# Channel mixers: one product, the plain blocks' last product and their low parts moved to GpSimd, and a third down slab converted later

## The chip, the cores and the metric

The kernel runs on one core of one Trainium2 chip. The metric is the time of one execution on the device, in microseconds (us); lower is better. The core's engines work from queues of their own, each in order: TensorE (PE) multiplies matrices, ScalarE (ACT) applies functions and converts, VectorE (DVE) and GpSimd (POOL) work element by element, and SyncE (SP) issues the transfers (DMA) from the large memory. An engine that needs another's result waits on a semaphore, and everything behind the waiting instruction in its own queue waits with it.

## The reference

A decoder trunk of two layers on 512 tokens of width 1024, all in float32. Each layer runs a channel mixer, a token mixer (latent attention in the first layer, sparse attention in the second) and a second channel mixer; a last norm closes the trunk.

```python
def rmsnorm(x, g):
    y = x32 * lax.rsqrt(jnp.mean(x32 * x32, axis=-1, keepdims=True) + RMS_EPS)
    return y.astype(x.dtype) * g
def swiglu(x, w_gate, w_up, w_down):
    return (jax.nn.silu(x @ w_gate) * (x @ w_up)) @ w_down
...
  h = h + 1/2 * SwiGLU_a(RMSNorm(h))
  h = h + Mixer_i(RMSNorm(h))
  h = h + 1/2 * SwiGLU_b(RMSNorm(h))
```

So there are four channel mixers (idx 0 to 3 below), with 2816 hidden values each. The change touches only these.

## The kernel before

**Two parts for each number.** Every float32 factor is kept as a high part, rounded by a copy on ACT (L176), and a low part, the difference, subtracted on DVE (L177); `split` makes both, and its argument `pool=True` gives the subtraction to POOL. A product takes three matmuls, high by high, high by low and low by high (`mm3`, `product`, `plain`).

**Blocks.** A channel mixer works through 22 blocks f of 128 hidden values, with all 512 tokens in the free dimension. The first 3 blocks of idx 0, and the first 2 of the others, are plain: gate and up are multiplied out directly (`plain`, L379 to L381) into the banks pg and pu. The others take one turn of the main loop each, in which gate and up together are made by seven half-sized products of sums (a Strassen scheme) in the order 1, 7, 6, 2, 5, 4, 3, into three banks px, pq and pg. `wsums` makes five weight sums for a later turn on DVE (L353, L354, L356, L357) from the raw slabs wr (called rg there) and ru and splits them. Within a turn ACT copies px to pg after product 1 (L496; product 6 then goes on in px, so PE waits for that copy), then pq and px to uq (L498, L500), and px to pg after product 5 (L503). DVE adds up the up half in tile tu (L504, L506).

**Activation.** `row` is a tile 128x512 that holds every token's norm factor. `gate` multiplies the gate by row (DVE, L395), applies silu with a turned sign (ACT, L396, tile tg) and multiplies the result by row once more (DVE, L397); that second product brings in the factor that the up half lacks. `act` multiplies tu by tg (L408 on DVE; for plain blocks L406, which reads the bank pu and turns the sign) and splits the result into ah (ACT) and al (DVE). `plain_acts` does both for the plain blocks, and stands behind the weight sums of the first turn.

**Down.** For every three finished blocks there are eight units, one for each 128 rows of the output: `unit` loads a down slab wdr (L425, SP), splits it into two wd tiles (ACT and DVE), runs nine matmuls into bank pd (L168 to L170) and adds the result to h (L419). They are spread over the next three turns as 3, 3 and 2, with the bank tags "o", "T" and "S"; only a turn's third unit has the tag "S". From `tail` = 18 on, the last blocks' turns are spread otherwise.

**What orders the work.** A scheduler places every instruction on its engine's queue from its own estimates. `issue_after(x)` keeps what it encloses behind instruction x on that engine. The tag "w2" (tu) has two buffers, "dr" (wdr) two, "wr" two, "dh" and "dl" (wd) three.

Of the kernel before, what the change touches and what calls it, by code (L numbers as in the profile page):

```python
# [14 lines left out]
AF = mybir.ActivationFunctionType  # L15
ALU = mybir.AluOpType
AX = mybir.AxisListType

P = 128
S = 512  # L20
# [27 lines left out]
HS = S // 2  # L48
# [16 lines left out]
class Kern:  # L65
# [317 lines left out]
    def ffn(self, idx, gain_next, ap, tp):  # L383
        nc, a = self.nc, self.a
        self.scr, self.fp = (tp, "sq", 1), tp
        ah, al, ht, plain = {}, {}, [], PLAIN[idx]
        self.nsum = 0
        ap.tile([P, 3 * PAD], F32, name="even")
        tp.tile([P, 5 * PAD], F32, name="odd", bufs=1)
        tg, tu, units = {}, {}, []  # L390

        def gate(f, g):

            t = tg[f] = tp.tile([P, S], F32, tag="tg", bufs=2, name="tg")
            nc.vector.tensor_tensor(t, g, row, op=ALU.mult)  # L395
            nc.scalar.activation(t, t, AF.Silu, scale=-1.0)  # L396
            nc.vector.tensor_tensor(t, t, row, op=ALU.mult)  # L397

        def tu_tile():
            return self.xp.tile([P, S], F32, tag="w2", bufs=2, name="tu")  # L400

        def act(f):
            t = tu[f]
            if f < plain:
                t = tu_tile()
                nc.vector.scalar_tensor_tensor(t, tu[f], -1.0, tg[f], op0=ALU.mult, op1=ALU.mult)  # L406
            else:
                nc.vector.tensor_tensor(t, t, tg[f], op=ALU.mult)  # L408
            ah[f] = ap.tile([P, S], F32R, tag="act", bufs=4 * NG, name="ah")
            al[f] = ap.tile([P, S], F32R, tag="act", bufs=4 * NG, name="al")  # L410
            self.split(t, ah[f], al[f])

        def down(p, w, b0, b1):
            for k in range(b0, b1):
                last = self.mm3(p, w[0][:, k - b0], w[1][:, k - b0], ah[k], al[k], k == b0, k == b1 - 1)
            return last

        def add(c, p):
            nc.vector.scalar_tensor_tensor(self.h[c], p, 0.5, self.h[c], op0=ALU.mult, op1=ALU.add)  # L419

        def unit(tag, b0, c):

            w = [ap.tile([P, NG * P], F32R, tag=t, bufs=3, name="wd").rearrange("p (k c) -> p k c", c=P) for t in ("dh", "dl")]
            raw = ap.tile([P, NG * P], F32, tag="dr", bufs=2, name="wdr")
            nc.sync.dma_start(raw, a["w_down"][idx, c, :, b0 * P : (b0 + NG) * P])  # L425
            self.split(raw.rearrange("p (k c) -> p k c", c=P), *w)
            p = self.bank(tag, "pd")
            down(p, w, b0, b0 + NG)
            add(c, p)

        sums, xts = self.small_sums, []

        def tokens(t):

            xts.append(tp.tile([P, D], F32, tag="fr", bufs=3, name="xt"))
            with self.tc.issue_after(self.high.ins):
                nc.scalar.dma_start(xts[t], a["x_tok"][t * P : (t + 1) * P, :])

        def squares(t):
            nc.scalar.activation(xts[t], xts[t], AF.Square, accum_out=sums[:, t : t + 1])  # L440

        if idx == 0:
            for t in range(3):
                tokens(t)


        def plain_acts():
            for e, g in enumerate(gates):
                gate(e, g)
                act(e)  # L450
            t = self.tiny
            for i, g in enumerate(gates[::-1]):
                nc.scalar.activation(t[:, i + 1 : i + 2], g[:, 0:1], AF.Identity, bias=t[:, i : i + 1])

        row = self.row_tile(tp, tag="row", bufs=1)
        gates = [self.bank("T", "pg") for _ in range(plain)]
        for f, g in enumerate(gates):
            u = tu[f] = self.bank(("mm", "S")[f % 2], "pu")
            self.plain(idx, f, 0, g)
            if f == 0 and idx:  # L460
                with self.tc.high_priority(URGENT):
                    for c in self.late:
                        self.sumsq(self.h[c])
                self.norm_col(D, self.s2, URGENT, col=row[:, 0:P:32])
                self.norm_row(row, URGENT)
            if f == 1 and idx == 0:

                squares(0)
                tokens(3)
                squares(1)  # L470
            self.plain(idx, f, 1, u)
            if f == 1 and idx == 0:
                squares(2)
                squares(3)
                self.rsqrt_col(sums, D, col=row[:, 0:P:32])
                self.norm_row(row)
            for p in (((0, 1), (2, 3)) if plain == 2 else ((0, 1), (2,), (3,)))[f]:
                self.combine(p)

        tail, left = (NF - 2) // NG * NG, 1  # L480
        for f in range(plain, NF):
            if f % NG == 0 and f <= tail:
                units = [partial(unit, b0=f - NG, c=c) for c in range(KC)]
                left = NG if f < tail else NF - tail
            n = -(-len(units) // left)
            left -= 1
            todo, units = units[:n], units[n:]
            w = self.wsums(idx, f)
            if f == plain:
                plain_acts()  # L490
            x, q, g = self.bank("S", "px")[:, :HS], self.bank("mm", "pq")[:, :HS], self.bank("T", "pg")
            uq = tp.tile([P, S], F32, tag="uq", bufs=1, name="uq")
            t = tu[f] = tu_tile()

            self.product(1, w, x, True, False)
            nc.scalar.activation(g[:, :HS], x, AF.Copy)  # L496
            self.product(7, w, q, True, False)
            nc.scalar.activation(uq[:, :HS], q, AF.Copy)  # L498
            self.product(6, w, x, False, False)
            nc.scalar.activation(uq[:, HS:], x, AF.Copy)  # L500
            self.product(2, w, g[:, :HS], False, True)
            self.product(5, w, x, False, True)
            nc.scalar.activation(g[:, HS:], x, AF.Copy)  # L503
            nc.vector.tensor_tensor(t[:, HS:], x, uq[:, :HS], op=ALU.add)  # L504
            self.product(4, w, q, False, True)
            nc.vector.tensor_tensor(t[:, :HS], q, uq[:, HS:], op=ALU.add)  # L506
            self.product(3, w, g[:, HS:], False, True)
            gate(f, g)
            for work, tag in zip(todo, "oTS"):
                work(tag)  # L510
            act(f)
        if gain_next == "fin":

            hs, out = [self.parts(self.four(F32)) for _ in range(4)], []
            for t in range(4):
                for b in range(2):
                    p = self.mm_bank("ph")
                    for c in range(4):
                        nc.tensor.transpose(p[:, c * P : (c + 1) * P], self.h[4 * b + c][:, t * P : (t + 1) * P], self.ident)
                    out.append(hs[t][b])  # L520
                    nc.scalar.activation(out[-1], p, AF.Copy)
            return self.last(a["w_last"], ah, al, ap, out, hs)
        self.norm_begin(gain_next)
        for c in self.order:
            p = self.mm_bank("pd")
            raw = tp.tile([P, D], F32, tag="fr", bufs=3, name="wdr")[:, : (NF - tail) * P]
            nc.sync.dma_start(raw, a["w_down"][idx, c, :, tail * P :])
            w = [t[:, o : o + (NF - tail) * P].rearrange("p (k c) -> p k c", c=P)
                 for t, o in zip(self.sum_tiles(1024), (3 * PAD, SHIFT[self.nsum % 3] * PAD))]
            self.split(raw.rearrange("p (k c) -> p k c", c=P), *w)  # L530
            down(p, w, tail, NF)
            add(c, p)
            self.norm_chunk(c)
# [910 lines left out]
```

## Time and profile before

| what | value |
|---|---|
| runs | 1862.45, 1862.96, 1863.68 us |
| median | 1862.96 us |
| profiled execution | 1862.92 us, of it the span in the trace 1861.1 us |
| PE busy | 1837.6 us, 99% |
| DVE busy | 1526.8 us, 82% |
| ACT busy | 1077.2 us, 58% |
| POOL busy | 251.3 us, 14% |
| transfers | 191.11 MB, mean 103 GB/s |

In the rows below, a group is read as: line, engine, operation, what is written and read (tile names without buffer numbers), shape and count, then busy time in us, the mean length of one in ns, and how long its engine stood idle before such instructions and for whom. A row of the timeline gives the start and length in us, then engine, line and operation, and in brackets the idle time ahead of it. A row of the view of waits gives a sum in us, how often, and the longest.

### The profile page before, as it was taken

Reading aid. Unit: us, or ns where it says so; the run is one execution under the profiler, and the core shown is the slowest. Engines: PE = TensorE matmul, PEld = TensorE weight load, DVE = VectorE, ACT = ScalarE, POOL = GpSimd, SP = SyncE. Lnnn points to the kernel's source line nnn. Section 1 sums busy time; section 2 is a strip of 40 time slices with the busy share of each in tenths; the row PEclk is TensorE's granted clock in tenths of the full one; section 3 lists DMA queues with packets and bytes.
Section 4 is the critical chain, followed back from the end, with each engine's and each line's share of the span. In section 5 each row is a group of like instructions: output and inputs, shape, how many; then the busy total and the mean of one; then the engine's idle time right before and its main releaser. Section 6 shows DMA issues by size and latency. Waiting matters only on the chain. (4 is left out here: it accounts for less than half of the span.)

```text
span 1861.1 us, 32606 instructions
## 1 busy us (share of the span) xinstructions
PE 1837.6 (99%) x12392; PEld 1676.7 (90%) x12392; DVE 1526.8 (82%) x2773; ACT 1077.2 (58%) x2030; POOL 251.3 (14%) x350
## 2 busy tenths in 40 slices
PE   8999999999999999999999999999999999999998
PEld 8999999888889999998999999888888889999997
DVE  7988886588789888877998888755988989988885
ACT  8545554489766545445654544426977865444554
POOL 0000000156510000000000000015665500000000
PEclk9999999999999999999999999999999999999999
DMA  7333333142333333323233332333232123333321
GB/s 258 122 103 102 103 97 115 55 109 68 99 126 102 110 111 109 108 92 105 87 128 105 106 103 91 96 105 108 75 86 74 46 105 125 114 107 102 102 83 64
DMA packets 79212, 191.11 MB, mean 103 GB/s; under 512 B 10024, under 2 KB 38080, under 8 KB 79056
## 3 DMA queue, kind: packets, MB, share of 16 engines
q1 hardware_dynamic: 75280, 182.42, 30.5%
q10 hardware_dynamic: 3104, 5.03, 0.8%
q8 instruction: 97, 1.59, 0.3%
q0 software_dynamic: 672, 1.59, 0.3%
q14 instruction: 59, 0.48, 0.1%
HBM read 179.75 MB, written 2.18 MB: 98 GB/s over the span
## 5 line engine op out<-in xcount | busy, mean ns | idle before, releaser
L169 PE MATMUL pd<-al,wd 128*128 128x512 f32 x576 | 224.4, 390 | 0.0
L170 PE MATMUL pd<-ah,wd 128*128 128x512 f32 x576 | 224.4, 390 | 0.0
L168 PE MATMUL pd<-ah,wd 128*128 128x512 f32 x576 | 224.3, 389 | 0.0
L367 PE MATMUL px<-four,wh 128*128 128x256 f32 x632 | 176.3, 279 | 5.2 <-ACT pg L496 5.2
L369 PE MATMUL px<-four,wl 128*128 128x256 f32 x632 | 175.3, 277 | 0.8 <-DVE wl L177 0.8
L367 PE MATMUL pq<-four,wh 128*128 128x256 f32 x632 | 174.9, 277 | 0.2 <-DVE tu L406 0.2
L368 PE MATMUL px<-four,wh 128*128 128x256 f32 x632 | 175.0, 277 | 0.0
L369 PE MATMUL pq<-four,wl 128*128 128x256 f32 x632 | 174.8, 277 | 0.0
L368 PE MATMUL pq<-four,wh 128*128 128x256 f32 x632 | 174.8, 277 | 0.0
L176 ACT ACTIVATE wd<-wdr 128x384 fp32r<-128x384 f32 x192 | 99.3, 519 | 104.4 <-issue 74.7
L419 DVE SCALAR_TENSOR_TENSOR h<-pd,h 128x512 f32<-128x512 f32 x216 | 147.8, 684 | 6.4 <-PE pd L170 6.4
L177 DVE TENSOR_TENSOR wl<-s,wh 128x512 fp32r<-128x512 f32 x79 | 54.5, 690 | 116.8 <-ACT wh L176 116.8
L176 ACT ACTIVATE wh<-s 128x512 fp32r<-128x512 f32 x79 | 49.8, 630 | 136.9 <-PE px L368 128.9
L170 PEld LDWEIGHTS pd<-ah,wd 128*128 128x128 f32 x576 | 108.2, 188 | 22.3
L168 PEld LDWEIGHTS pd<-ah,wd 128*128 128x128 f32 x576 | 108.2, 188 | 19.4
L169 PEld LDWEIGHTS pd<-al,wd 128*128 128x128 f32 x576 | 108.1, 188 | 19.4
L367 PEld LDWEIGHTS px<-four,wh 128*128 128x128 f32 x632 | 118.7, 188 | 7.5 <-ACT pg L496 7.0
L369 PEld LDWEIGHTS px<-four,wl 128*128 128x128 f32 x632 | 118.7, 188 | 1.2 <-DVE wl L177 1.2
L367 PEld LDWEIGHTS pq<-four,wh 128*128 128x128 f32 x632 | 118.7, 188 | 0.3 <-ACT w L176 0.3
L368 PEld LDWEIGHTS px<-four,wh 128*128 128x128 f32 x632 | 118.7, 188 | 0.0
L368 PEld LDWEIGHTS pq<-four,wh 128*128 128x128 f32 x632 | 118.7, 188 | 0.0
L369 PEld LDWEIGHTS pq<-four,wl 128*128 128x128 f32 x632 | 118.7, 188 | 0.0
(366 smaller groups left out, 6017.1 us busy)
## 6 DMA issues: line engine op xcount, KB each, us to landing
wr<-in_w_gu SPq DMA_DIRECT2D x93, 512.0 KB, 3.2
ru<-in_w_gu SPq DMA_DIRECT2D x79, 512.0 KB, 4.2
wdr<-in_w_down SPq DMA_DIRECT2D x192, 192.0 KB, 2.5
wdr<-in_w_down SPq DMA_DIRECT2D x24, 256.0 KB, 3.0
wr<-in_mla_w_o SPq DMA_DIRECT2D x8, 512.0 KB, 3.6
wr<-in_nsa_w_q SPq DMA_DIRECT2D x8, 512.0 KB, 3.6
th<-btab_d SPq DMA_DIRECT2D x16, 256.0 KB, 3.4
wr<-in_nsa_w_o SPq DMA_DIRECT2D x8, 512.0 KB, 3.5
```

The lines of the kernel that those rows point to most:

```text
L168: mm(out, wh, xh, start=first, stop=False)
L169: mm(out, wh, xl, start=False, stop=False)
L170: return mm(out, wl, xh, start=False, stop=last)
L176: nc.scalar.activation(hi, src, AF.Copy)
L177: (nc.gpsimd if pool else nc.vector).tensor_tensor(lo, src, f32v(hi), op=ALU.subtract)
L367: mm(out, wh[:, p], xh, start=first and p == 0, stop=False, skip_group_check=True)
L368: mm(out, wh[:, p], xl, start=False, stop=False, skip_group_check=True)
L369: mm(out, wl[:, p], xh, start=False, stop=last and p == KP - 1, skip_group_check=True)
L419: nc.vector.scalar_tensor_tensor(self.h[c], p, 0.5, self.h[c], op0=ALU.mult, op1=ALU.add)
```

## The change

`gate` loses its second product by row. In a turn, a new product (L506 in the changed kernel) multiplies the up half tu by row, behind the two adds that make it, on POOL for the turns before `tail` and on DVE for the rest. In a plain block DVE forms minus the up half times row into a tile of its own, from the bank pu (L447), and POOL does both the product with tg (L403) and the subtraction that gives al. The split of a turn's third down slab is kept behind the ACT copy of product 5 (`copied`, now L502). The changed kernel's lines are five lower in `act` and `unit` (product L403, add L414, transfer L420), one lower in the loop (copies L495, L497, L499, L502; adds L503, L505).

```diff
@@ gate, act
             nc.scalar.activation(t, t, AF.Silu, scale=-1.0)
-            nc.vector.tensor_tensor(t, t, row, op=ALU.mult)
...
-            if f < plain:
-                t = tu_tile()
-                nc.vector.scalar_tensor_tensor(t, tu[f], -1.0, tg[f], op0=ALU.mult, op1=ALU.mult)
-            else:
-                nc.vector.tensor_tensor(t, t, tg[f], op=ALU.mult)
+            (nc.gpsimd if f < plain else nc.vector).tensor_tensor(t, t, tg[f], op=ALU.mult)
...
-            self.split(t, ah[f], al[f])
+            self.split(t, ah[f], al[f], pool=f < plain)
@@ unit
-        def unit(tag, b0, c):
+        def unit(tag, behind, b0, c):
...
-            self.split(raw.rearrange("p (k c) -> p k c", c=P), *w)
+            with self.tc.issue_after(behind.ins) if behind else nullcontext():
+                self.split(raw.rearrange("p (k c) -> p k c", c=P), *w)
@@ plain_acts
                 gate(e, g)
+                v = tu_tile()
+                nc.vector.scalar_tensor_tensor(v, tu[e], -1.0, row, op0=ALU.mult, op1=ALU.mult)
+                tu[e] = v
                 act(e)
@@ the turn
-            nc.scalar.activation(g[:, HS:], x, AF.Copy)
+            copied = nc.scalar.activation(g[:, HS:], x, AF.Copy)
...
+            (nc.gpsimd if f < tail else nc.vector).tensor_tensor(t, t, row, op=ALU.mult)
             self.product(3, w, g[:, HS:], False, True)
             gate(f, g)
             for work, tag in zip(todo, "oTS"):
-                work(tag)
+                work(tag, copied if tag == "S" else None)
```

On ACT, at the entry of idx 1 (behind the plain blocks; s, ru, rg and wr are raw weights and their sums, four a token sum, and w and wh high parts), there stands before:

```order
L176 ACTIVATE wh<-ru 128x1024
L396 ACT_TABLE_LOAD
L396 ACTIVATE tg<-tg 128x512
L176 ACTIVATE wh<-rg 128x1024
L396 ACTIVATE tg<-tg 128x512
L453 ACTIVATE gains<-pg,gains 128x1
L176 ACTIVATE w<-wr 128x1024
L453 ACTIVATE gains<-pg,gains 128x1
L496 ACTIVATE pg<-px 128x256
L176 ACTIVATE ah<-tu 128x512
```

and now, at the same place:

```order
L176 ACTIVATE wh<-ru 128x1024
L396 ACT_TABLE_LOAD
L396 ACTIVATE tg<-tg 128x512
L176 ACTIVATE wh<-rg 128x1024
L176 ACTIVATE ah<-tu 128x512
L396 ACTIVATE tg<-tg 128x512
L452 ACTIVATE gains<-pg,gains 128x1
L176 ACTIVATE w<-wr 128x1024
L452 ACTIVATE gains<-pg,gains 128x1
L495 ACTIVATE pg<-px 128x256
```

The first plain block's ah, which stood behind the copy out of px, now stands ahead of it, and its source tu is written by POOL.

On DVE, in a turn with three units in the middle of idx 1 (the one whose L504 runs at 646.81 us), there stands before:

```order
L504 TENSOR_TENSOR tu<-px,uq 128x256
L506 TENSOR_TENSOR tu<-pq,uq 128x256
L353 TENSOR_TENSOR s_7928<-ru 128x512
L177 TENSOR_TENSOR wl<-wr,wh 128x1024
L395 TENSOR_TENSOR tg<-pg,row 128x512
L177 TENSOR_TENSOR wl<-ru,wh 128x1024
L397 TENSOR_TENSOR tg<-tg,row 128x512
L419 SCALAR_TENSOR_TENSOR h_94<-pd,h_94 128x512
L408 TENSOR_TENSOR tu<-tu,tg 128x512
```

and now:

```order
L505 TENSOR_TENSOR tu<-pq,uq 128x256
L177 TENSOR_TENSOR wd<-wdr,wd 128x384
L353 TENSOR_TENSOR s_7928<-ru 128x512
L395 TENSOR_TENSOR tg<-pg,row 128x512
L177 TENSOR_TENSOR wl<-wr,wh 128x1024
L403 TENSOR_TENSOR tu<-tu,tg 128x512
L414 SCALAR_TENSOR_TENSOR h_94<-pd,h_94 128x512
L177 TENSOR_TENSOR wd<-wdr,wd 128x384
L177 TENSOR_TENSOR al<-tu,ah 128x512
L414 SCALAR_TENSOR_TENSOR h_95<-pd,h_95 128x512
L177 TENSOR_TENSOR wd<-wdr,wd 128x384
L177 TENSOR_TENSOR wl<-ru,wh 128x1024
```

The low part of ru's sum (wl from ru), which the next turn's product 7 reads, has moved from behind L395 to behind the second unit's add; a wd now stands ahead of L353. In a turn with two units wl from ru stays where it was, and only L397 is gone.

On POOL, the first piece of difference in its queue, at idx 0 (3 plain blocks, then 15 turns):

```order
 L291 DMA nrow<-row 4x4x32
 L293 DMA row<-nrow 128x512
+L403 TENSOR_TENSOR tu<-tu,tg 128x512
+L177 TENSOR_TENSOR al<-tu,ah 128x512
+L403 TENSOR_TENSOR tu<-tu,tg 128x512 x2
+L177 TENSOR_TENSOR al<-tu,ah 128x512 x2
+L506 TENSOR_TENSOR tu<-tu,row 128x512 x15
 L304 MEMSET row 128x128
 L282 TENSOR_TENSOR row<-small,gains 128x4
```

POOL had nothing between the row's transfers and the next norm; now it has 21 instructions there, and 20 in each of the other three channel mixers.

## The prediction

> **What bounds the kernel now.** I read the engines' shares first, then the slices, then what PE waits for.
>
> ```profile
> PE 1837.6 (99%) x12392; PEld 1676.7 (90%) x12392; DVE 1526.8 (82%) x2773; ACT 1077.2 (58%) x2030; POOL 251.3 (14%) x350
> DVE  7988886588789888877998888755988989988885
> POOL 0000000156510000000000000015665500000000
> ```
>
> PE is busy in 99% of the span, so a faster engine elsewhere can only give back PE's waits. DVE is busy to eight or nine tenths in the channel mixers (slices 1 to 7, 13 to 18, 20 to 25 and 34 on), and POOL is idle there: its digits are zero. The view of waits tells how much PE loses:
>
> ```profile
> PE pg L379 <- ACT w L149: 5.9, 1, 5.9
> PE px L367 <- ACT pg L496: 5.2, 6, 2.1
> PE pg L367 <- ACT pg L503: 1.3, 3, 0.5
> PE px L369 <- DVE wl L177: 0.8, 2, 0.6
> PE pq L367 <- DVE tu L406: 0.2, 1, 0.2
> ACT wd L176 <- DMA wdr<-in_w_down: 23.0, 35, 3.4
> ```
>
> The first row is the start of the program, which the change leaves alone. The next four lie in the channel mixers: 5.2 + 1.3 + 0.8 + 0.2 = 7.5 us, 0.40% of the span. That is all the change can win. What it can lose has no such limit, since any of 79 turns can begin to wait.
>
> **The third slab's conversion.** The longest of those waits is one place, at the entry of idx 2:
>
> ```profile
> 916.52 0.52 ACT L176 ACTIVATE wd<-wdr 128x384 fp32r<-128x384 f32 x1 [3.44 <-DMA wdr<-in_w_down]
> 917.47 0.36 ACT L496 ACTIVATE pg<-px 128x256 f32<-128x256 f32 x1
> ```
>
> ACT stood 3.44 us before a slab that had not landed, and the copy that PE's product 6 needs stood two behind it. With that conversion kept behind the copy of product 5, ACT reaches L496 earlier, and the wait's 2.1 us go. What is late next there is ah of the plain block, below. In the other turns the third slab's conversion moves from behind L496 to behind L502, with no added instruction; the 23.0 us of ACT's waits are nearly all idle time of an engine busy to 58%, so I cost that at nothing. The slabs have more time to land, which covers SP's new order, in which ru's transfer stands behind three wdr of a turn.
>
> **The second product by row.** DVE loses 88 products L397 and gets 16 back (the blocks from 18 on); POOL gets 63.
>
> ```profile
> L397 DVE TENSOR_TENSOR tg<-tg,row 128x512 f32<-128x512 f32 x88 | 60.2, 686 | 3.1 <-ACT tg L396 2.6
> L406 DVE SCALAR_TENSOR_TENSOR tu<-pu,tg 128x512 f32<-128x512 f32 x9 | 6.0, 682 | 0.0
> L177 DVE TENSOR_TENSOR al<-tu,ah 128x512 fp32r<-128x512 f32 x88 | 60.7, 690 | 7.5 <-ACT ah L176 7.1
> L155 POOL TENSOR_TENSOR w<-wr,w 128x512 fp32r<-128x512 f32 x43 | 55.8, 1317 | 43.7 <-ACT w L149 43.2
> L177 POOL TENSOR_TENSOR qr<-tq,qr 128x512 fp32r<-128x512 f32 x6 | 7.7, 1302 | 0.2 <-ACT qr L176 0.2
> ```
>
> DVE's account is (88 - 16) x 0.686 = 49.4 us less for the products, 9 x 0.69 = 6.2 us less for the plain blocks' al, and nothing for L406, since nine L447 of its form take its place: 56 us in all, 3% of the span. By itself that is worth at most the 7.5 us above. POOL's price is that of the same kind and size, 1.30 to 1.32 us. In a turn it has time: tu is ready when the last add ends and is needed about 3 us later, by the product with tg. At 1.3 us that is hidden.
>
> The Trainium skill, page GPSIMD Engine Reference, section 3.1, has such an operation of 2048 elements a lane at 4497 ns on GpSimd; an estimate from it for 512 is 1124 ns. The rows above have 1302 and 1317, and by the page's figure the turns below would lose some 0.2 us less each; the rows decide.
>
> **What DVE and POOL do to each other.** That cost is seen elsewhere in this trace, in the sparse mixer, where both work at once:
>
> ```profile
> 1419.57 2.57 POOL L155 TENSOR_TENSOR w<-wr,w 128x512 fp32r<-128x512 f32 x2
> 1419.29 0.69 DVE L1234 TENSOR_TENSOR npt<-pt,npt 128x512 fp32r<-128x512 f32 x1 [0.27 <-ACT npt L1233]
> 1420.80 1.89 DVE L1033 TENSOR_TENSOR q<-t,q 64x512 fp32r<-64x512 f32 x1 [0.36 <-ACT q L1032]
> L1033 DVE TENSOR_TENSOR q<-t,q 64x512 fp32r<-64x512 f32 x5 | 6.0, 1197 | 0.5 <-ACT q L1032 0.4
> ```
>
> At 1420.80 DVE begins an operation whose two inputs both lie in SBUF (t and q). It takes 1.89 us instead of 0.69, and ends about 0.55 us after POOL's second product does, at 1422.14: it has stood still until POOL was through. The operation at 1419.29, with one input in PSUM (pt), runs beside POOL's first at its ordinary 0.69. So a POOL product costs DVE up to its own 1.3 us if DVE meets it with an operation on two SBUF tiles, and nothing if DVE is then at one with a PSUM input. In the channel mixers most of DVE's work is of the first kind (L353, L354, L356, L357, all low parts, the product with tg); L395, L504, L506 and the adds L419 are of the second. Moving 0.69 us off DVE can thus put up to 1.3 us on it.
>
> **A turn with two units.** Here is one of before:
>
> ```profile
> 662.80 0.41 DVE L506 TENSOR_TENSOR tu<-pq,uq 128x256 f32<-128x256 f32 x1
> 663.13 0.68 DVE L353 TENSOR_TENSOR s<-ru 128x512 f32<-128x512 f32 x1
> 663.73 1.22 DVE L177 TENSOR_TENSOR wl<-wr,wh 128x1024 fp32r<-128x1024 f32 x1
> 664.98 0.33 SPq L332 DMA_DIRECT2D wr<-in_w_gu  x1
> 668.36 1.05 ACT L176 ACTIVATE w<-wr 128x1024 fp32r<-128x1024 f32 x1
> 669.84 0.37 ACT L496 ACTIVATE pg<-px 128x256 f32<-128x256 f32 x1
> 670.64 0.28 PE L367 MATMUL px<-four,wh 128*128 128x256 f32 x1
> wr<-in_w_gu SPq DMA_DIRECT2D x93, 512.0 KB, 3.2
> ```
>
> When wl from wr ends (664.95), SP sends for the next wr; it lands some 3.2 us later (last row, the median of all), is converted at 668.36, and the copy L496 stands behind that conversion on ACT. PE needs the copy for the matmul at 670.64. In the changed kernel POOL's product can start once the second add ends, at 663.21, with L353 already running; it gets its turn at 663.8 and holds up wl from wr until 665.1, which ends at 666.3 instead of 664.95. The transfer goes out 1.35 us later, so w is converted from about 669.7 to 670.75 and the copy starts then; product 6 could start at about 670.9, 0.3 us late. If DVE gets in first, wl runs on time and POOL comes afterwards, beside L395: nothing lost. There are 5 such turns in each channel mixer ahead of block 18, 20 in all. Between 0 and 0.3 I take 0.15: 20 x 0.15 = +3.0 us.
>
> **A turn with three units.** The low part of ru now stands late in DVE's order. Its steps, by the starts of a turn of before:
>
> ```profile
> 647.15 0.41 DVE L506 TENSOR_TENSOR tu<-pq,uq 128x256 f32<-128x256 f32 x1
> 647.48 0.68 DVE L353 TENSOR_TENSOR s<-ru 128x512 f32<-128x512 f32 x1
> 648.08 1.22 DVE L177 TENSOR_TENSOR wl<-wr,wh 128x1024 fp32r<-128x1024 f32 x1
> 649.21 0.69 DVE L395 TENSOR_TENSOR tg<-pg,row 128x512 f32<-128x512 f32 x1
> 653.35 1.02 DVE L177 TENSOR_TENSOR wd<-wdr,wd 128x384 fp32r<-128x384 f32 x2
> 655.89 0.28 PE L369 MATMUL pq<-four,wl 128*128 128x256 f32 x1
> 661.86 0.69 DVE L177 TENSOR_TENSOR wl<-s,wh 128x512 fp32r<-128x512 f32 x1 [2.73 <-ACT wh L176]
> ```
>
> From start to start a 512-wide operation takes 0.60, a 1024-wide one 1.13, a wd about 0.48. In the new order, from 647.48: wd, L353, L395, wl from wr, the product with tg, an add, wd, al, an add, wd, and then wl from ru. That is 3 x 0.48 + 6 x 0.60 + 1.13 = 6.17, so wl from ru starts at 653.65 and ends at 654.87. PE reads it at 655.89: 1.0 us to spare. POOL's product falls between wd and L353 and costs 0.5 (if L353 goes first and L395 covers part of it) to 1.3 us. So these 40 turns come out between 0.5 to spare and 0.3 late; I take nothing, and keep 40 x 0.3 = 12 us for the range. The 2.73 us that DVE idles at each turn's end (last row) absorbs the rest, so the delay does not add up over turns.
>
> **The four entries.** Before, at idx 1:
>
> ```profile
> 565.49 0.63 ACT L396 ACTIVATE tg<-tg 128x512 f32<-128x512 f32 x1
> 566.71 1.06 ACT L176 ACTIVATE wh<-rg 128x1024 fp32r<-128x1024 f32 x1 [0.59 <-DVE rg L357]
> 567.67 0.61 ACT L396 ACTIVATE tg<-tg 128x512 f32<-128x512 f32 x1
> 569.57 0.39 ACT L496 ACTIVATE pg<-px 128x256 f32<-128x256 f32 x1
> 570.01 0.39 PE L367 MATMUL px<-four,wh 128*128 128x256 f32 x1 [0.60 <-ACT pg L496]
> ```
>
> Here ACT is already late: PE waits 0.60 for the copy. Now ah of the first plain block stands ahead of the second silu, and its source is POOL's: silu ends at 566.12, POOL's product 1.3 us later at 567.5 if POOL gets in at once, ah follows the weight copy at about 567.7, and silu and copy move back by an ah, some 0.6 us; if POOL must first let one of DVE's operations pass (0.7 to 1.2 us), by up to 1.4. The copy is thus 0.6 to 2.0 us later. I take 1.3 at each of four entries, +5.2 us (the rest reach the copy by like orders; at idx 0 it is a down matmul that waits for the plain blocks' ah and al). Against it go the waits that the shorter DVE line and the slab's new place remove: 2.1 for the slab, and of the other 5.4 us two thirds, 3.4, as the entries that keep waiting count anew: -5.5 us.
>
> Then DVE's own line there. It loses 2 x 0.69 for L397 and 2 x 0.69 for al, and may stand still for four POOL operations, 4 x 1.31: 2.5 us more backlog at worst, 3.7 with three plain blocks, 11.2 in all, and at best 12.3 us less backlog. The entries of before have PE waiting for DVE's wl (0.8 us), so backlog reaches PE there, but only in part. I take a quarter of the worst, +2.8.
>
> **Sum.** +3.0 + 0 + 5.2 - 5.5 + 2.8 = +5.5 us on the profiled execution's 1862.92 (0.04 below the median of the runs): 1868.4, rounded to 1868.
>
> **The rivals.**
> - *POOL slips in where DVE does not mind.* Then no turn waits, the entries' +5.2 and -5.5 cancel, and it is 1862.6, no change. For it: 2.73 us of idle DVE in a turn, the PSUM operations around the product, and 1.0 us to spare for ru. Against: the row of 1.89 us.
> - *The waits go and nothing comes instead*, faster: DVE's 56 us less work shorten its backlog at the entries and most of 7.5 us return: 1862.9 - 6 = 1857. It needs POOL's two products at an entry to cost the copy nothing, that is, the scheduler's estimate of POOL to be true there; it is decided at the copy at 569.57: if that comes no later than now, this holds. Against it: POOL's 1.3 us stands on ACT's path.
> - *Every POOL operation stops DVE for its whole length*: turns with three units late by 0.2 (40 x 0.2 = 8), with two by 0.3 (6), entries 5: 1862.9 + 19 - 0.3 = about 1882. Against it: DVE's order has a PSUM operation within two steps of each POOL product.
>
> The Trainium skill, page SBUF — State Buffer, section Who interferes with whom, states the rule behind this last rival: a DVE instruction with two SBUF inputs contends with a GpSimd instruction that reads SBUF, and the second to issue waits for the whole of the first. The row of 1.89 us agrees; how often the two meet in the channel mixers, no run here shows yet.
>
> **How the numbers follow.** The forecast, a few us lost, has 0.36; no change 0.33; faster 0.21; the last rival 0.10. A measurement of this kernel tells 0.2%, 3.7 us, from no change: below 1859.2 is faster, above 1866.7 slower. The forecast's own range, 1865 to 1873, reaches a little under that bound, and so does no change go over it: faster 0.21, same 0.35, slower 0.44. The range takes the faster case in to 1857 and the bad one to 1877.
>
> **What would show it.** In the changed kernel's trace: the wait of 3.44 us before wd at the entry of idx 2 is gone. POOL's products in turns take about 1.3 us alone and up to 2.5 when they wait for DVE; L353 or wl from wr shows means well over 682 and 1218 ns. PE's waits for ACT's pg L495 (6 before, as L496) grow in number to 20 or more, each about 0.2 us, if the turns with two units wait; waits for wl at product 7 appear if those with three do. If instead DVE's means stay as they are, the term for two units and the entries' 2.8 are wrong, and the time is at or under 1863. If the copies at the entries come no later, the +5.2 is wrong.

## The result, and the profile after

The changed kernel takes 1891.11 us (median of four runs, 1890.55 to 1893.12), the kernel before 1863.32 us beside it: 27.8 us slower, a ratio of 1.0149 (95% interval 1.0131 to 1.0166). The forecast was 1868.0, the range 1857 to 1877: the sign was right, the size five times too small, and the range did not hold it.

The shares of the engines and the slices of POOL, on the page of the changed kernel:

```profile
PE 1851.9 (98%) x12392; PEld 1685.5 (89%) x12392; DVE 1562.1 (83%) x2692; ACT 1080.3 (57%) x2030; POOL 379.3 (20%) x431
POOL 1200000056511001100211000015666501000000
```

DVE has 81 instructions fewer and is busy for 35 us longer, where the prediction's account had it 56 us lighter. The groups show which instructions grew (last columns: busy us, mean ns, idle us before), first two of the kernel before, then the changed one's:

```profile
L177 DVE TENSOR_TENSOR wl<-wr,wh 128x1024 fp32r<-128x1024 f32 x76 | 92.6, 1218 | 2.4 <-ACT wh L176 2.3
L353 DVE TENSOR_TENSOR s<-ru 128x512 f32<-128x512 f32 x79 | 53.9, 682 | 0.4 <-DMA ru<-in_w_gu 0.4
```

```profile
L177 DVE TENSOR_TENSOR wl<-wr,wh 128x1024 fp32r<-128x1024 f32 x76 | 120.7, 1588 | 0.0
L353 DVE TENSOR_TENSOR s<-ru 128x512 f32<-128x512 f32 x79 | 92.9, 1176 | 0.8 <-DMA ru<-in_w_gu 0.8
L506 POOL TENSOR_TENSOR tu<-tu,row 128x512 f32<-128x512 f32 x63 | 98.4, 1562 | 817.3 <-DVE tu L505 799.8 <-ACT wh L176 12.7 <-issue 4.8
L403 POOL TENSOR_TENSOR tu<-tu,tg 128x512 f32<-128x512 f32 x9 | 14.2, 1577 | 46.7 <-DVE tu L447 26.3 <-PE pu L381 11.5 <-ACT tg L396 8.8
L177 POOL TENSOR_TENSOR al<-tu,ah 128x512 fp32r<-128x512 f32 x9 | 14.4, 1607 | 5.6 <-ACT ah L176 5.6
```

L353 went from 682 to 1176 ns and wl from wr from 1218 to 1588: 79 x 0.494 + 76 x 0.370 = 67 us of standing still in these two lines alone. By the trace, 79 DVE operations beside the 81 POOL operations are longer than their like, by 81.5 us in all or some 1.0 us each; not one of them reads a bank of PSUM. What PE waited for:

```profile
PE px L367 <- ACT pg L495: 12.8, 11, 2.5
PE px L367 <- ACT uq L499: 3.7, 3, 1.7
PE pd L168 <- ACT ah L176: 1.2, 1, 1.2
PE pg L367 <- ACT pg L502: 1.1, 1, 1.1
PE px L369 <- DVE wl L177: 0.5, 2, 0.3
```

That is some 19 us, against 7.5 before; a wait in one of the turns is mostly too short for this view (0.3 us). So I also took every turn's length from the starts of the first matmul of product 1 in both traces and summed the differences by kind of turn. "Entry" is the plain blocks of a channel mixer and its turns up to block 5; "after a short one" are turns that follow one with two units, "second" the other turns with three units, "two units" those with two, "last" the turns from block 18 on (the first of them, turn 18, also follows one with two units). In us, with the medians' ratio to the kernel before:

| kernel | entries | after a short one | second | two units | last | ratio (95%) |
|---|---|---|---|---|---|---|
| changed | +18.8 | +5.1 | 0.0 | +3.9 | +1.7 | 1.0149 (1.0131 to 1.0166) |
| turns' product on DVE | +12.9 | +3.6 | 0.0 | 0.0 | +2.1 | 1.0096 (1.0081 to 1.0111) |
| plain blocks on DVE | +6.7 | +5.7 | +0.3 | +5.5 | +2.5 | 1.0100 (1.0084 to 1.0115) |
| all on DVE | +1.1 | +4.2 | 0.0 | 0.0 | +2.3 | 1.0023 (1.0010 to 1.0036) |
| changed, no late slab | +21.5 | +5.5 | +17.5 | +22.7 | +2.1 | 1.0371 (1.0354 to 1.0389) |
| changed, turns' product left out | +12.3 | -1.9 | 0.0 | +0.5 | +0.3 | 1.0050 (1.0034 to 1.0066) |
| before, late slab only | -0.3 | -1.5 | 0.0 | +0.2 | 0.0 | 0.9985 (0.9975 to 0.9994) |
| before + product a turn | +8.6 | +11.5 | +0.8 | +0.2 | +3.2 | 1.0105 (1.0087 to 1.0123) |
| before + two operations a plain block | +23.2 | -1.3 | 0.0 | 0.0 | 0.0 | 1.0118 (1.0102 to 1.0133) |

These are differences of single profiled executions. Two executions of the kernel with the late slab only differ by up to 0.7 us at one entry, and a kernel below that takes the same time as the one before (1.0001, the product with a column) has +2.5 at its entries; differences of that size there say little.

**The entry, in the changed kernel.** The timeline at idx 1, POOL, ACT, DVE and PE put in order of time:

```profile
577.60 1.30 POOL L403 TENSOR_TENSOR tu<-tu,tg 128x512 f32<-128x512 f32 x1 [11.40 <-DVE tu L447]
577.97 2.02 DVE L177 TENSOR_TENSOR w<-wr,w 128x1024 fp32r<-128x1024 f32 x1
578.93 0.63 ACT L176 ACTIVATE ah<-tu 128x512 fp32r<-128x512 f32 x1 [0.92 <-POOL tu L403]
579.91 2.29 DVE L177 TENSOR_TENSOR wl<-rg,wh 128x1024 fp32r<-128x1024 f32 x1
581.36 0.38 ACT L495 ACTIVATE pg<-px 128x256 f32<-128x256 f32 x1
581.80 0.58 PE L367 MATMUL px<-four,wh 128*128 128x256 f32 x1 [2.51 <-ACT pg L495]
582.94 1.60 POOL L403 TENSOR_TENSOR tu<-tu,tg 128x512 f32<-128x512 f32 x1 [1.83 <-DVE tu L447]
583.32 2.30 DVE L177 TENSOR_TENSOR w<-wr,w 128x1024 fp32r<-128x1024 f32 x1
```

POOL's product ends at 578.90 and ah, silu, w and the copy follow; PE waits 2.51 us for that copy, where it waited 0.60. Each POOL operation stretches a DVE operation of 1.22 us to 2.0 to 2.3. Then something follows that the prediction did not have. The stretches around it (the third number from the end is the granted clock):

```profile
580.00:582.00 2.00, 0.20 (x1) 0.21 (x2) 2.00 (x1) 1.98 (x6) 1.11 (x1) 0.92 0.00 0
582.00:584.00 2.00, 2.00 (x10) 2.00 (x11) 2.00 (x4) 0.04 (x1) 1.06 (x1) 0.50 0.38 96
584.00:586.00 2.00, 2.00 (x15) 2.00 (x15) 2.00 (x2) 1.42 (x3) 1.26 (x2) 0.73 0.43 166
```

After the wait PE's granted clock (the share of its full clock that it gets) is 0.50 for about 3.4 us, and its matmuls start every 0.21 us instead of every 0.113. There are four such stretches, one at the longest wait of each entry; half of 3.41 us is lost in each, 6.8 us in all. The kernel before has none among its matmuls. So of the entries' 18.8 us up to 6.8 are a slower PE, and the rest waits. ACT, which makes the copies, waits for POOL's product at these places:

```profile
ACT ah L176 <- POOL tu L403: 12.9, 8, 2.5
```

**A turn after one with two units.** The timeline in idx 1:

```profile
634.02 1.62 POOL L506 TENSOR_TENSOR tu<-tu,row 128x512 f32<-128x512 f32 x1 [14.18 <-DVE tu L505]
634.39 2.33 DVE L177 TENSOR_TENSOR wl<-wr,wh 128x1024 fp32r<-128x1024 f32 x1
636.75 0.33 SPq L332 DMA_DIRECT2D wr<-in_w_gu  x1
640.23 1.05 ACT L176 ACTIVATE w<-wr 128x1024 fp32r<-128x1024 f32 x1
641.18 0.37 ACT L495 ACTIVATE pg<-px 128x256 f32<-128x256 f32 x1
641.60 0.39 PE L367 MATMUL px<-four,wh 128*128 128x256 f32 x1
```

This is the forecast's turn, step by step: POOL's product starts while L353 runs and is through first, wl from wr takes 2.33 us instead of 1.22, the next wr is sent 1.1 us late, w and the copy follow, and product 6 starts 0.3 us late.

### The profile page after: what moved, and what is told of

Read it like the earlier page. It is cut to its first block, busy times and chain, and to the rows that moved or that the text cites. A ratio compares the mean times of both kernels' runs of the same rounds, so it can differ in the third digit from the quotient of the medians.

```text
span 1889.5 us, 32840 instructions
## 1 busy us (share of the span) xinstructions
PE 1851.9 (98%) x12392; PEld 1685.5 (89%) x12392; DVE 1562.1 (83%) x2692; ACT 1080.3 (57%) x2030; POOL 379.3 (20%) x431
## 4 chain that ended last, share of the span: by engine, by line
PE 73%; DVE 17%; ACT 5%; DMA 2%; issue 2%; POOL 1%; DVEq 0%; SPq 0%; ACTq 0%; POOLq 0%
PE pd L170 6%; PE pd L168 6%; PE pd L169 6%; DVE wl L177 6%; PE px L367 5%; PE px L368 5%; PE px L369 4%; PE pg L367 3%; PE pg L369 3%; PE pg L368 3%; PE pq L368 2%; PE pq L369 2%; PE pq L367 2%; PE o L1247 2%; PE pt L1222 2%
## 5 line engine op out<-in xcount | busy, mean ns | idle before, releaser
L506 POOL TENSOR_TENSOR tu<-tu,row 128x512 f32<-128x512 f32 x63 | 98.4, 1562 | 817.3 <-DVE tu L505 799.8
L367 PE MATMUL px<-four,wh 128*128 128x256 f32 x632 | 180.9, 286 | 19.0 <-ACT pg L495 12.8
L368 PE MATMUL px<-four,wh 128*128 128x256 f32 x632 | 176.6, 279 | 0.0
L414 DVE SCALAR_TENSOR_TENSOR h<-pd,h 128x512 f32<-128x512 f32 x216 | 146.7, 679 | 8.8 <-PE pd L170 8.8
L177 DVE TENSOR_TENSOR wl<-wr,wh 128x1024 fp32r<-128x1024 f32 x76 | 120.7, 1588 | 0.0
L176 ACT ACTIVATE w<-wr 128x1024 fp32r<-128x1024 f32 x75 | 79.4, 1059 | 68.9 <-DMA wr<-in_w_gu 66.6
```

The costliest lines, as they stand in the source:

```text
L176: nc.scalar.activation(hi, src, AF.Copy)
L177: (nc.gpsimd if pool else nc.vector).tensor_tensor(lo, src, f32v(hi), op=ALU.subtract)
L367: mm(out, wh[:, p], xh, start=first and p == 0, stop=False, skip_group_check=True)
L368: mm(out, wh[:, p], xl, start=False, stop=False, skip_group_check=True)
L506: (nc.gpsimd if f < tail else nc.vector).tensor_tensor(t, t, row, op=ALU.mult)
```

## The experiments

**Which part costs what.** Five kernels undo or isolate parts.

```diff
-            (nc.gpsimd if f < tail else nc.vector).tensor_tensor(t, t, row, op=ALU.mult)
+            nc.vector.tensor_tensor(t, t, row, op=ALU.mult)
```

> The changed kernel with the turns' product of the up half by row on DVE in all 79 turns; the plain blocks' POOL work and the late third slab stay. Theory A (a DVE operation on two SBUF tiles and a POOL operation exclude each other): the late starts in turns, some 10 of the 28 us lost, go, the loss at the four entries (about 19 us) stays: about 1881 us, L353 back to 0.68 us. Rival B (the new order of DVE's and ACT's work, whatever POOL does): the turns still wait, and DVE has 43 us more: 1891 us or more.

1881.89 us, 9 us less than the changed kernel. The total is theory A's, but not its places, so the agreement is luck: the turns after a short one are still 0.2 to 0.4 us late each in 14 of 16, and the entries came down from 18.8 to 12.9. On DVE, the product and behind it L395 stand ahead of wl from wr, which in the turns with two units starts 2.1 us after the second add instead of 0.9, so 1.2 us late. In the changed kernel only L353 stands there in most of these turns, and POOL makes wl from wr 1.1 us longer. Two causes, one delay.

```diff
-            (nc.gpsimd if f < plain else nc.vector).tensor_tensor(t, t, tg[f], op=ALU.mult)
+            nc.vector.tensor_tensor(t, t, tg[f], op=ALU.mult)
...
-            self.split(t, ah[f], al[f], pool=f < plain)
+            self.split(t, ah[f], al[f])
```

> The changed kernel with the plain blocks' product with tg and their al on DVE; POOL keeps the turns' product by row. Theory A: the four entries come back to about the time of before, less what the late third slab wins (2 to 4 us), and the turns' 10 us stay: about 1870 us, no hold over 2 us left and so no fall of the granted clock. Rival B: the entries' order is what costs, 1885 us or more.

1882.51 us: between the two theories. The entries fell by 12 us and the stretches of half clock are gone from them, but 6.7 us stay there: POOL's product by row also costs time in an entry's first turns (the runs below that remove it or add it alone put it at 6.5 and 8.6 us there).

Both edits together:

> The changed kernel with all products and low parts on DVE, so that only the earlier place of the product by row, the plain blocks' new tile and the late third slab are left of the change. Theory A: nearly all of the loss is POOL's: 1861 to 1866 us. Rival: the product's earlier place by itself holds up the low part of wr and with it the next turn (the run with the turns' product on DVE still had late turns): 1868 us or more.

1869.23 us. Without any new POOL work the change still costs about 4 us (1.9 to 6.7 by the interval; the profiled execution is 6.8 longer): by the table 4.2 in the turns after a short one, 2.3 in the last turns and 1.1 in the entries. The rival was right on the turns, theory A on the entries. So giving the products and low parts to POOL and not to DVE costs 27.8 - 4.3 = 23.5 us in this order. The 4.2 us are no part of the changed kernel's 5.1: there DVE has no product in these turns, and without POOL's product they lose nothing (below). Taken one at a time, the plain blocks' part is 13.6 us (the run with the turns' product on DVE, +17.9, less 4.3) and the turns' part 14.3 (+18.6 less 4.3). Why these come to 27.9 together and not 23.5 is open; each has an interval of nearly 3 us either way, and at the entries the parts do add up (11.8 + 5.6 against 17.7).

```diff
-                work(tag, copied if tag == "S" else None)
+                work(tag, None)
```

> The changed kernel without the late third slab; all POOL work stays. If the slab's place wins 2 us there too: about 1893 us. Rival: the late slab is what pushes DVE's low part of ru late and makes turns wait: about 1881 us.

1931.85 us, 41 us worse than with the late slab: both expectations missed. What PE and ACT waited for, and one place:

```profile
PE px L367 <- ACT pg L495: 39.3, 42, 2.2
ACT wd L176 <- DMA wdr<-in_w_down: 71.3, 35, 3.6
664.55 0.52 ACT L176 ACTIVATE wd<-wdr 128x384 fp32r<-128x384 f32 x1 [1.95 <-DMA wdr<-in_w_down]
664.98 0.37 ACT L495 ACTIVATE pg<-px 128x256 f32<-128x256 f32 x1
```

The edit also changes DVE's order: POOL now meets wl from wr in nearly every turn (2059 ns in the mean, 1588 in the changed kernel), so wr, ru and behind them the slabs are sent late. In the order that the scheduler makes here, the third slab's conversion stands ahead of the copy L495: ACT waits for it there, and PE for ACT. With the late slab ACT's waits for wdr are 7.0 us in all. Late slabs alone do not cost this much. The kernel before with one more POOL product a turn, below, has wl from wr at 2002 ns and these waits of ACT and PE:

```profile
ACT wd L176 <- DMA wdr<-in_w_down: 59.8, 41, 3.6
PE px L367 <- ACT pg L496: 15.8, 25, 2.2
```

But its third conversion stands behind that copy, as in the kernel before, and its "second" and "two units" turns lose 1.0 us together, against 40.2 here. So the 41 us point to the place ahead of the copy, which the late slab rules out; they do not show that a place behind product 5 is better than one behind product 1. The late slab alone, on the kernel before:

```diff
-            self.split(raw.rearrange("p (k c) -> p k c", c=P), *w)
+            with self.tc.issue_after(behind.ins) if behind else nullcontext():
+                self.split(raw.rearrange("p (k c) -> p k c", c=P), *w)
```

> The kernel before with the third slab's conversion kept behind the copy of product 5, and nothing else. By the prediction's term: the wait of 3.44 us before wd goes and with it the 2.1 us that PE waited, about 1860 to 1861 us. Rival: the other orders that the scheduler makes with it lose as much, 1863 us or more.

1861.5 us, ratio 0.9985 (0.9975 to 0.9994): the only version that beats the kernel before. It was run again, beside a variant that keeps the slab behind the copy of product 1 instead.

> The kernel before with the third slab's conversion behind the copy of product 5 once more, in more rounds, beside the other: 1861.5 us, 0.1 to 0.2% under the kernel before, if the first measurement holds.

> The kernel before with the third slab's conversion kept behind the turn's first copy (of product 1) in place of the copy of product 5. In most turns it stood there anyway, so the order hardly moves; the wait of 3.44 us before that copy at the entry of idx 2 goes. If that wait is the only thing the late slab wins: 1861 us, with fewer new waits than with the copy of product 5. If the wait only moves behind the copy and meets the next one: 1863 us.

Again 0.9989 (0.9981 to 0.9998), 1861.16 us; the variant 0.9992 (0.9982 to 1.0002), not told from no change. The waits of the repeated run:

```profile
PE px L367 <- ACT pg L497: 2.3, 4, 0.8
PE pg L367 <- ACT pg L504: 1.5, 4, 0.6
```

The waits for the first copy went from 5.2 to 2.3 us, the 2.1 us at idx 2 among them. But the turn behind that place became 0.6 to 0.9 us longer in the two traces, so that the entry of idx 2 won only 1.1 to 1.2; 1.5 more came from turns after a short one.

**The exclusion by itself.** Five kernels add or remove only POOL's work; in all of them PE, DVE, ACT and SP have the same instructions in the same order as the kernel that they are compared with.

```diff
             nc.vector.tensor_tensor(t[:, :HS], q, uq[:, HS:], op=ALU.add)
+            if f < tail:
+                extra = tp.tile([P, S], F32, tag="extra", bufs=1, name="extra")
+                nc.gpsimd.tensor_tensor(extra, t, row, op=ALU.mult)
```

> The kernel before, with one more POOL product of tu by row in each of the 63 turns ahead of block 18, into a tile that nothing reads; the queues of the other engines hold the same instructions in the same order as before. Theory A (exclusion): L353 or wl from wr takes 1.1 us longer in each of these turns, the next wr is sent for 1.1 us later, and turns wait: 1870 to 1885 us. Rival (only waiting for POOL's result, or the new order, costs time): 1863 us.

1884.29 us: 20 us for 63 products that nobody reads. Here it is wl from wr that stands still, 0.78 us in the mean:

```profile
L509 POOL TENSOR_TENSOR extra<-tu,row 128x512 f32<-128x512 f32 x63 | 104.6, 1661 | 884.0 <-DVE tu L506 868.6 <-DVE tu L504 15.3
L177 DVE TENSOR_TENSOR wl<-wr,wh 128x1024 fp32r<-128x1024 f32 x76 | 152.2, 2002 | 2.3 <-ACT wh L176 2.3
```

Nothing waits for the unread tile, and no queue but POOL's has changed, so neither latency nor order can be the cause of these 20 us. The next two ask which POOL work does this. In one the product is replaced by one of a single column and two fills of the tile:

```diff
+                nc.gpsimd.tensor_tensor(extra[:, :1], t[:, :1], row[:, :1], op=ALU.mult)
+                nc.gpsimd.memset(extra, 0.0)
+                nc.gpsimd.memset(extra, 0.0)
```

> As the run with one more POOL product a turn, but POOL makes a product of one column, to start at the same time, and then fills the unread tile twice, an operation without an input in SBUF and together at least 0.8 us long. If the exclusion is between two SBUF inputs on DVE and POOL's reading (what the Trainium skill's page SBUF - State Buffer, section Who interferes with whom, states): DVE's means as before, 1863 us. If any POOL work stops DVE: as the run with the product.

In the other by a product with one column:

```diff
+                nc.gpsimd.tensor_scalar(extra, t, row[:, :1], None, op0=ALU.mult)
```

> As the run with one more POOL product in each of the 63 turns, but tu is multiplied by one column (a tensor_scalar, one SBUF tile read), into the unread tile; all other queues as before. If POOL's reading of one SBUF tile is enough to stop DVE's operations on two: L353 and wl from wr longer by about that operation's own length, some 0.7 to 0.9 us, 1870 to 1880 us. If only POOL's second input does it: 1863 us.

1864.07 us (1.0002, 0.9993 to 1.0012) and 1864.93 us (1.0001, 0.9991 to 1.0010): no cost from either that an interval of 0.1% shows. The groups of the fills first, then of the product with a column:

```profile
L510 POOL MEMSET extra<- 128x512 f32 x63 | 33.3, 529 | 3.7
L177 DVE TENSOR_TENSOR wl<-wr,wh 128x1024 fp32r<-128x1024 f32 x76 | 92.6, 1218 | 2.4 <-ACT wh L176 2.3
```

```profile
L509 POOL TENSOR_SCALAR extra<-tu,row 128x512 f32<-128x512 f32 x63 | 178.3, 2831 | 798.6 <-DVE tu L506 784.1 <-DVE tu L504 14.5
L177 DVE TENSOR_TENSOR wl<-wr,wh 128x1024 fp32r<-128x1024 f32 x76 | 92.6, 1218 | 2.3 <-ACT wh L176 2.3
L353 DVE TENSOR_TENSOR s<-ru 128x512 f32<-128x512 f32 x79 | 53.9, 682 | 0.3 <-DMA ru<-in_w_gu 0.3
```

DVE's means are those of before to the nanosecond. The second time is that of "only POOL's second input does it", but POOL reads a whole tile there, and it is POOL that is long (2831 ns in the mean, from 1575 to 3003), not DVE. One turn of it:

```profile
647.25 0.68 DVE L353 TENSOR_TENSOR s<-ru 128x512 f32<-128x512 f32 x1
647.50 2.92 POOL L509 TENSOR_SCALAR extra<-tu,row 128x512 f32<-128x512 f32 x1 [12.74 <-DVE tu L506]
647.85 1.22 DVE L177 TENSOR_TENSOR wl<-wr,wh 128x1024 fp32r<-128x1024 f32 x1
```

It ends 1.35 us after wl from wr. In 62 of the 63 turns the product ends 1.35 to 1.44 us after the end of a DVE operation on two SBUF tiles, wherever it began; the 63rd, which began while DVE was at L395 with its input in PSUM, took the 1575 ns. So POOL seems to wait here until DVE is through, and lets an operation that starts after it (wl from wr) go first. Why it gives way in this form, and how long the form takes away from DVE, was not run.

The changed kernel without the turns' product on POOL (the factor is left out in those turns):

> The changed kernel without POOL's product by row in the 63 turns: that factor of the up half is left out there, everything else stands in the same order on every engine. Theory A: what the turns lost beside POOL goes, 9 to 10 us, and the entries' 19 us stay: about 1881 us. Rival (order and latency, not POOL): 1889 us or more.

1873.73 us, 17.4 less and 7 under theory A, more than what the turns had lost: the turns are back to the time of before and the entries fell from 18.8 to 12.3, since the product also costs time in an entry's turns. And the plain blocks' POOL work added to the kernel before, twice a block, unread:

```diff
             self.split(t, ah[f], al[f])
+            if f < plain:
+                for _ in range(2):
+                    extra = tp.tile([P, S], F32, tag="extra", bufs=1, name="extra")
+                    nc.gpsimd.tensor_tensor(extra, t, f32v(ah[f]), op=ALU.subtract)
```

> The kernel before, with two more POOL operations for each of the 9 plain blocks (tu minus its high part, twice, into a tile that nothing reads), all other queues as before. It adds the POOL work of the plain blocks without anything that waits for it. The runs so far put that work at about 12 us, with the exclusion and the wait for POOL's result together. If DVE's standing still is most of it: 1870 to 1876 us. If the wait for POOL's result on ACT's way to the copy is most of it, as the prediction's entry term had it: 1864 to 1867 us.

1885.51 us, 22 us for 18 operations, all of it at the entries and more than both expectations had:

```profile
PE px L367 <- ACT pg L500: 10.8, 6, 4.1
L415 POOL TENSOR_TENSOR extra<-tu,ah 128x512 f32<-128x512 f32 x18 | 30.3, 1682 | 60.4 <-ACT ah L176 59.4
```

Nothing waits for POOL's result in this kernel. It keeps all of DVE's own work, which the changed kernel does not, so it is not the changed kernel's entry; but it shows that DVE's standing still, 18.3 us in all, is enough to lose this much there: 1.2 us for each operation, with PE's slower clock in it (four stretches again, up to 6.8 us). In the changed kernel the standing still and ACT's wait for POOL's product come together at an entry, and no run parts them there.

## Why the prediction was wrong, point by point

- **The entries' DVE backlog ("I take a quarter of the worst, +2.8") and the copies there ("I take 1.3 at each").** These two terms failed, and with them the credit of 5.5 that stood against them. The entries were to come to +2.5; they measure +18.8. The mechanism was named rightly, the sizes were far too small. At idx 1 the three DVE rows quoted above stood still for 0.8, 1.07 and 1.08 us, and L354 for 1.1 more: 4.05 us for four POOL operations, where the worst case was 4 x 1.31. A DVE that is behind starts its next operation at once, and POOL met one each time. The copy there, taken at 1.3 us, made PE wait 2.51 us instead of 0.60. Of the credit, the late slab's part came in part and the shorter DVE line's did not show: all on DVE, the entries are at +1.1. How the loss divides between DVE's standing still and ACT's wait for POOL's product (12.9 us in eight waits) is open; the unread operations show that the first alone is enough.
- **PE's clock.** The prediction had no term for it: up to 6.8 us of the entries' 18.8.
- **Turns with two units (+3.0).** The mechanism was right, the size too small: in 18 of the 20 turns behind them (turn 18 included) the turn is 0.27 to 0.49 us longer, 0.43 in the mean, above the bound of 0.3. That bound was itself too low: the prediction has product 6 start 0.15 us after the copy does, but in its own rows of the entry 0.44 us lie between them (569.57 to 570.01). The prediction missed that the product on DVE would hold up the same turns (+4.2 with no POOL work at all), and that the turns with two units sometimes wait themselves (+3.9, in four turns): in three of these ACT waits 0.8 to 1.7 us for a slab just then.
- **Turns with three units (0).** Right, 0.0: L353 stood still for 1.1 us, as bounded (1176 against 682 in the mean over all turns), and the sixteen second turns kept their length to 0.1 us.
- **"DVE's account is 56 us less."** Wrong by sign, +35 us busy, since 81.5 us of standing still came in; without it DVE would be 46 us lighter, near the account. POOL's price of 1.30 us for one operation was right (577.60 above), but 1562 to 1607 in the mean beside DVE.
- **The late slab.** The wait of 2.1 us at idx 2 went, but 0.6 to 0.9 us came back in the next turn and 1.5 were won elsewhere, so that the total (0.9985 and 0.9989 by itself) agrees partly by luck. "I cost that at nothing" held on the kernel before; beside the POOL work, the scheduler's order without it costs 41 us.
- **The last turns.** The +1.7 is turn 18, behind a turn with two units (+1.7, and 0.0 without POOL's product); turn 19, behind the first of the 16 products that stay on DVE, lost 1.2 more, for which the prediction had no term, and turn 20 won 1.2 back.
- **What would show it.** L353 and wl from wr grew and the wait of 3.44 us went, as said; PE's waits for the copy L495 grew to 11 and not to 20, as most of the turns' are too short for the view.
- **The rivals.** "Every POOL operation stops DVE for its whole length", 0.10, came nearest (1882), but put the loss into the turns. The rule of the Trainium skill, page SBUF — State Buffer, section Who interferes with whom, named beside it, agrees with POOL's products of two tiles (2002 instead of 1218 ns) and with the fills that read nothing (1218). With the product with a column the one that waits is POOL, although DVE's operation starts later, so who waits does not follow from who issues first there.

## What to carry to other kernels

The price of moving an element-wise product of two tiles from DVE to POOL is not POOL's time but what DVE loses beside it: here 0.69 us taken off DVE put about 1.0 back on, wherever DVE worked back to back on pairs of SBUF tiles. Look first at the neighbours of the moved operation, and if the trace holds one place where both engines meet, price every meeting at its full length where DVE is behind. A constraint on the order that wins 2 us alone can be worth 41 beside another change, because without it the scheduler chose a worse order there; so undo parts one by one before judging a bundle.

## What the runs showed of the hardware that was not expected

- A fill on POOL (529 ns, no input) and a product with one column (2831 ns in the mean, one tile read) left DVE's operations on two SBUF tiles at 1218 and 682 ns; a product or difference of two tiles made them up to 2.33 us. The product with a column seems to stand back for DVE instead.
- PE's granted clock can fall to 0.50 for 3.41 us after a wait of some two microseconds, and where the wait lies matters as much as its length. By the clock records, all such stretches of one execution begin on a grid of 3.413 us: in the changed kernel at 83.33, 581.67, 926.42 and 1561.30 us, which are 146, 101 and 186 steps apart. Here are two windows of that grid, each with the next one, in the kernel before and in the changed one, both at the entry of idx 2 (length, PE busy, clock):

```profile
913.49:916.90 3.41, 2.34 (x21) 1.00 0.68 208
916.90:920.31 3.41, 2.42 (x21) 1.00 0.34 117
```

```profile
923.01:926.42 3.41, 1.52 (x13) 1.00 0.33 131
926.42:929.83 3.41, 3.41 (x19) 0.50 0.19 58
```

The first kernel's wait of 2.06 us (915.84 to 917.90) is shared by two windows, and nothing follows; the second's of 1.89 us lies in one, and the clock falls. In the fourteen traces, behind the first 20 us, each of the 29 windows in which PE stood idle for 1.94 us or more was followed by a stretch at half clock, none with less than 1.65 us was, and of 13 between them 7 were; what decides between is open. So it is partly chance how many of the entries' waits cost clock. The Trainium skill, page TensorE: Matmul & The Clock Gate, section Part 1, has the clock halved after an idle window of about 3.4 us. The length of the stretches and the step of the grid agree with that figure; that the whole window must be idle does not: 1.65 to 2.7 us in it were enough.
